# A two-layer hybrid diffusion trunk on one core: first norm's modulation split nine tiles on TensorE and seven rows on VectorE, later rows moved, out projection's low parts on GpSimd

## The chip, the core and the metric

One core of a Trainium2 chip runs the whole program in one launch. The metric is the device time in microseconds (us) of one execution; the median of three executions of the kernel before is 3165.7 us (3162.52 to 3169.48).

## The reference, cut to what matters

Two trunk layers act on 1024 latent tokens and 256 context tokens of width 1024. In each layer a conditioning vector is put through silu and a 1024 x 6144 matrix. It gives six vectors of 1024: shift, scale and gate of the mixing sub-layer, and shift, scale and gate of the MLP. Latent tokens use `c`, context tokens use `c_ctx`, with the same matrix.

```
mod   = split(silu(c)     @ w_mod[i] + b_mod[i], 6)     # sh1 sc1 ga1 sh2 sc2 ga2
mod_c = split(silu(c_ctx) @ w_mod[i] + b_mod[i], 6)
h = rmsnorm(x, g_pre_mix) * (1 + sc1) + sh1
u = h @ w_in                   # short conv | latent attention | conformer conv | 2-D attention
x = x + ga1 * rmsnorm(concat(mixers(u)) @ w_out, g_post_mix)
hm = rmsnorm(x, g_pre_mlp) * (1 + sc2) + sh2
x = x + ga2 * rmsnorm(square(relu(hm @ w_mlp1)) @ w_mlp2, g_post_mlp)
```

## The kernel before, in words

Activations lie with features on the 128 partitions and tokens along the free axis, in three segments: latents 0 to 511 (segment 0), latents 512 to 1023 (segment 1) and the context (segment 2, 256 tokens). Every large product is made in three passes (`mm3`, L125): high weight by high activation, high by low, low by high. The weight's high part is made by ScalarE (`hilo`, L101), its low part by a subtraction (L102) that goes to VectorE or to GpSimd. `weights` (L104) chooses by a counter: `eng = nc.vector if self.wcount % 4 < self.walt else nc.gpsimd`. `self.walt` is 0 except in the output projections: `WALT[0]` holds for the two halves of segment 0's projection in each layer (L1063 to L1069), `WALT[1]` for those of segments 1 and 2 of layer 0 and the end of the first MLP there (L1090 to L1108).

**The modulation of layer 0.** The 6144 outputs are 48 groups of 128, here called rows: 0 to 7 the shift, 8 to 15 the scale and 16 to 23 the gate of the mixing norm, 24 to 47 the three of the MLP (its gate is 40 to 47). A row is made in one of three ways. `mod_pe` (L250) loads a 128 x 1024 tile of 512 KB and multiplies it on TensorE by both vectors, two columns wide, in eight matmuls (L258). `mod_rows` (L286) loads the transposed weights in halves of 256 KB and lets VectorE make one 128x512 product with accumulation (L300) for each half and each of the two vectors: four per row. `mod_whole` (L307) loads 512 KB at once; with two vectors it takes two 128x512 products (L319) and one of 128x1024 (L322). Its loads and products are pinned behind what was traced before them on their engine. `mod_rows` and `mod_whole` need the vectors on all partitions; `mod_vectors` (L265) makes them either by TensorE (a column of ones by a 4 KB row, L276, then silu, L277) or by a load that repeats the 4 KB row on all partitions, 512 KB of data, and a silu in place (L280, L282).

**The start** (`run`, L1175). Rows 0 to 6 (`MPE` = 7) are TensorE's and 7 to 15 VectorE's. `merge(self.mod_pe(early), (md, RM))` (L1233) runs them side by side. Behind the fifth tile (`MX` = 4) `early` loads segment 0, takes its sums of squares and its 1/rms, and loads the first weights. Segments 1 and 2 are loaded when row 15 has been written out in the program. The norm's scaling (`modulate`, L184: L200, L201, L202 for each of eight feature tiles) waits for rows 0 to 15 through `gains` (L338, L353).

**Layer 0** (`layer`, L1013). `merge(main, (other, rate), ...)` (L994) writes out the main generator's steps and, after each, steps of the others up to `rate` times the cost so far. Rows 16 to 47 (`moda`, L1025) go beside six stages in a row: segment 0's first projections together with the norms of segments 1 and 2 (`pend`), two gated projections, the values, the latent attention's projections and its heads. Beside them runs the 31-tap convolution (L442). Row loads use the tag `xl`, of three buffers. A list scheduler then orders each engine's queue by priority and by a simulated readiness, so an instruction can move ahead of the place where it was written. After the heads come attention and output projection of segment 0 (`outproj`, L889; norms `na`, `n2`), segments 1 and 2 in the same way, and the MLP. In the MLP of segments 1 and 2 (L1127) a generator `hn` runs beside the products: the last norm of segment 0 (`resa`), the 48 rows of layer 1 (`modc`, by `mod_whole`) and the first norm of layer 1.

All loads go out on SyncE's queue. The tag `s` has 20 buffers of 4 KB per partition, for modulation tiles first and for the normalized activations after.

Of the kernel before, what the change touches and what calls it, by code (L numbers as in the profile page):

```python
# [6 lines left out]
AF = mybir.ActivationFunctionType  # L7
# [19 lines left out]
HB = 2  # L27
QTAG = 'xl'
PA, PD = 0, 1
WALT = (3, 2)  # L30
MPE, RM, MX = 7, 1.0, 4
ROT0, ROT1, ROT2 = 'SGSGS', 'SGSGS', 'SGSGS'
RATES = dict(pend=(1.0, 1.0), cv=(1.0, 0.862), cp=(1.0, 0.6), hr=(1.0, 0.484), hc=(0.3, 0.3), hm=(0.313, 0.679), ma=(0.195, 0.26), mf=(0.5, 0.5), mv=(0.5, 1.04), cb=(1.0, 1.3), mp=(0.5, 0.5), ar=(0.392, 0.517), ac=(0.6, 0.8), ob=(0.65, 0.696), oc=(0.575, 0.65), od=(0.65, 0.26), on=(0.6, 0.522), mb=(1.0, 0.646), pr=(0.2, 0.2), pt=(0.805, 1.12), pn=(0.612, 1.5), pm=(1.5, 1.5), mn=(1.74, 2.0), mc=(0.29, 0.325), mt=(1.0, 0.6), en=(1.0, 1.0))
PADC = 15
CFW = PADC + LAT + PADC + CTX + PADC
T5 = 1328
# [33 lines left out]
class Kern:  # L70
# [176 lines left out]
        return self.tc.keep_in_program_order(ins)  # L247


    def mod_pe(self, load):  # L250

        nc = self.nc
        ps = self.ps("O", [P, MPE, 2])
        for m in range(MPE):
            raw = self.t([P, KT, P], "s")
            nc.sync.dma_start(raw, self.a["wmod0"][m])
            for k in range(KT):
                nc.tensor.matmul(ps[:, m, :], raw[:, k, :], self.sc[:, k, :], start=k == 0, stop=k == KT - 1)  # L258
            if m == MX:
                load()  # L260
            yield 1.0
        for v in range(2):
            nc.vector.tensor_tensor(self.mods[0][v][:, 0:MPE], ps[:, :, v], self.vec[:, 0, 0:MPE], op=ALU.add)

    def mod_vectors(self, tags, pe=False):  # L265

        nc = self.nc
        out = []
        for v in range(2):
            t = self.t([P, 2, 512], tags[v])  # L270
            if pe:
                row = self.t([1, 1024], "s")
                nc.sync.dma_start(row, self.a["crow"][v:v + 1, :])
                for h in range(2):
                    ps = self.ps("S")
                    nc.tensor.matmul(ps, self.ones[0:1, :], row[:, h * 512:(h + 1) * 512], start=True, stop=True)  # L276
                    nc.scalar.activation(t[:, h], ps, AF.Silu)  # L277
                out.append([t[:, 0], t[:, 1]])
                continue
            nc.sync.dma_start(t, self.a["crow"][v:v + 1, :].rearrange("v (h c) -> v h c", h=2)  # L280
                              .to_broadcast([P, 2, 512]))
            nc.scalar.activation(t, t, AF.Silu)  # L282
            out.append(Halves(t))
        return out
# [728 lines left out]
    def layer(self, l, H, pend):  # L1013

        last = l == 1
        R = {k: v[l] for k, v in RATES.items()}
        qsegs = (0, 1) if last else (0, 1, 2)
        bsegs = qsegs[1:]
# [3 lines left out]
        ch = self.chain  # L1022
        self.cf_open(0)
        self.cf_open(1)
        moda = self.mod_rows(0, 16, 48, self.vecs) if l == 0 else iter(())  # L1025
        first = ch(*[self.cf_gemm(l, H, (0,), j, j == 0 and l == 0) for j in range(2)], self.na_project(l, H, "NQ", M_NAQ, (0,)))
        if l:
            first = ch(first, self.na_project(l, H, "NK", M_NAK, (0,)))
        self.merge(first, (pend, R['pend']), (moda, R['ma']))
        self.go(pend)  # L1030
        self.merge(self.cf_gemm(l, H, bsegs, 0), (moda, R['mf']))
        conv = ch(*[self.cf_conv(l, qsegs, j) for j in range(2)])
        self.merge(self.cf_gemm(l, H, bsegs, 1), (conv, R['cb']), (moda, R['mf']))
        self.merge(self.values(l, H), (conv, R['cv']), (moda, R['mv']))
        self.mla_open()
        self.merge(self.mla_project(l, H, (0, 1, 2), qsegs), (conv, R['cp']), (moda, R['mp']))
        heads = self.mla_heads(l, qsegs)
        rest1 = ch(self.na_project(l, H, "NK", M_NAK, (1, 2) if l else (0, 1, 2)), self.na_project(l, H, "NQ", M_NAQ, bsegs))
        self.merge(heads, (rest1, R['hr']), (conv, R['hc']), (moda, R['hm']))
        self.go(moda)  # L1040
        self.rot = "G"
        self.yfalloc(0)
# [19 lines left out]
        HM = {}  # L1062
        self.walt = WALT[0]  # L1063
        self.merge(self.outproj(l, 0, 0, 256, y0), (attb, R['ob']))
# [45 lines left out]
        vecs = self.mod_vectors(("c5", "ah"))  # L1110
        modc = ch(self.mod_whole(1, 0, 16, vecs), self.mod_whole(1, 16, 48, vecs[:1]))
        HN = {}
        m = self.mlp(l, (1, 2), HM, "ah", {1: "c5", 2: "ya"}, [(1, 0, 512), (2, 0, 256)], nb)
# [4 lines left out]
            return t  # L1118

        def hn():  # L1120
            yield from resa
            yield from modc
            HN[0] = self.newh(512)
            yield from self.modulate(get0, 512, 1, "1", 0, HN[0], 0, tmp="T")

        hn = hn()
        self.merge(self.upto(m, "part"), (nb, R['mn']), (hn, R['mc']))  # L1127
        self.go(nb, hn)
        p1 = self.norm(self.macc[1], 1, 0, 512, l, "2", None, self.scr["XM"], xout, (1, "1", lambda: HN[1]), **free)
# [33 lines left out]
    @staticmethod  # L1163
    def stats(g):

        next(g)
        next(g)
# [7 lines left out]
    def run(self):  # L1175
        nc, tc = self.nc, self.tc
# [38 lines left out]
        def load(si, tag):  # L1215
            o, n = SEGS[si]
            X[si] = Seg(pools[tag], n, F32, tag, f"x{si}")
            for i, t in enumerate(X[si].tiles):
                kk = X[si].kk
                nc.sync.dma_start(t, a["xin"][:, i * kk:(i + 1) * kk, o:o + n])  # L1220

        self.vecs = self.mod_vectors(("ya", "ya"), True)
        md = self.mod_rows(0, MPE, 16, self.vecs, wtag="s")
        H, first = {}, []

        def early():
            load(0, "ah")
            g = self.modulate(X[0].k, 512, 0, "1", 0, lambda: H[0], 0, tmp="T")
            self.stats(g)
            first.append(g)  # L1230
            self.w0 = [self.weights(a["win"][0, m], D) for m in (M_CFG, M_CFA)]

        self.merge(self.mod_pe(early), (md, RM))  # L1233
        self.go(md)
        load(1, "c5")
        load(2, "ah")
# [2 lines left out]
        pend = self.chain(*[self.modulate(X[si].k, SEGS[si][1], 0, "1", int(si == 2), H[si], 0, ptag="O", tmp="T") for si in (1, 2)])  # L1239
        H, pend = self.layer(0, H, pend)  # L1240
# [104 lines left out]
```

## Time and profile before

| | us |
|---|---|
| median of 3 executions | 3165.7 |
| the profiled execution: device time | 3172.64 |
| the profiled execution: span, first to last instruction | 3170.7 |
| TensorE busy | 2962.9 (93%) |
| VectorE busy | 1978.2 (62%) |
| ScalarE busy | 1388.2 (44%) |
| GpSimd busy | 1095.1 (35%) |

A busy share over the whole span hides that the stages have different limits, so the stages are read one by one. A stage is a stretch of time; in its row the engines' busy times are compared with its length. In a row of the profile, L300 is line 300 of the kernel, `ma<-xl,ya` the tile written and the tiles read, and the releaser of an idle stretch is the work that ended last before the engine went on. The profiled execution is 6.9 us longer than the median, and what is added to or taken from it is taken to change the median by as much.

### The profile page before, as it was taken

Reading aid. Unit: us, or ns where it says so; the run is one execution under the profiler, and the core shown is the slowest. Engines: PE = TensorE matmul, PEld = TensorE weight load, DVE = VectorE, ACT = ScalarE, POOL = GpSimd, SP = SyncE. Lnnn points to the kernel's source line nnn. Section 1 sums busy time; section 2 is a strip of 40 time slices with the busy share of each in tenths; the row PEclk is TensorE's granted clock in tenths of the full one; section 3 lists DMA queues with packets and bytes.
Section 4 is the critical chain, followed back from the end, with each engine's and each line's share of the span. In section 5 each row is a group of like instructions: output and inputs, shape, how many; then the busy total and the mean of one; then the engine's idle time right before and its main releaser. Section 6 shows DMA issues by size and latency. Waiting matters only on the chain.

```text
span 3170.7 us, 45433 instructions
## 1 busy us (share of the span) xinstructions
PE 2962.9 (93%) x15720; PEld 2529.0 (80%) x15720; DVE 1978.2 (62%) x3964; ACT 1388.2 (44%) x2840; POOL 1095.1 (35%) x865
## 2 busy tenths in 40 slices
PE   7889889979999989999999998997889999999997
PEld 5777678878888888888888886876878788888886
DVE  8999555686663367566654788556766526344335
ACT  3313445676553355322222533555755434343332
POOL 1302113224544432333332512222324444444443
PEclk9889889989999999999999999998989999999998
DMA  7435423353542263534522534335534324234223
GB/s 265 153 121 190 123 60 104 113 158 100 153 122 97 97 200 100 177 116 168 185 81 80 173 108 165 101 84 138 172 89 148 104 97 143 97 104 139 94 97 103
DMA packets 273193, 405.77 MB, mean 128 GB/s; under 512 B 27074, under 2 KB 124354, under 8 KB 272964
## 3 DMA queue, kind: packets, MB, share of 16 engines
q1 hardware_dynamic: 272964, 402.87, 39.9%
q8 instruction: 125, 2.05, 0.3%
q14 instruction: 104, 0.85, 0.1%
HBM read 350.47 MB, written 52.30 MB: 127 GB/s over the span
## 4 chain that ended last, share of the span: by engine, by line
PE 76%; DVE 5%; DMA 3%; issue 2%; ACT 2%; SPq 1%; POOL 0%; DVEq 0%; ACTq 0%; POOLq 0%
PE G L130 12%; PE G L131 12%; PE G L132 12%; PE S L130 10%; PE S L132 9%; PE S L131 9%; PE T L715 3%; PE O L728 1%; PE O L727 1%; DMA ah<-KR 1%; PE S L849 1%; PE S L799 1%; PE S L798 1%; PE S L800 1%; DVE sm L685 1%
## 5 line engine op out<-in xcount | busy, mean ns | idle before, releaser
L102 POOL TENSOR_TENSOR wl<-raw,wh 128x512 fp32r<-128x512 f32 x676 | 916.4, 1358 | 1479.7 <-ACT wh L101 1358.5
L101 ACT ACTIVATE wh<-raw 128x512 fp32r<-128x512 f32 x752 | 473.0, 631 | 870.2 <-PE S L131 390.9
L130 PE MATMUL G<-h,wh 128*128 128x512 f32 (+1 forms) x1144 | 436.5, 382 | 3.9 <-ACT h L201 1.2
L131 PE MATMUL G<-h,wh 128*128 128x512 f32 (+1 forms) x1144 | 432.4, 378 | 4.4 <-DVE h L202 4.3
L132 PE MATMUL G<-h,wl 128*128 128x512 f32 (+1 forms) x1144 | 432.7, 378 | 0.2 <-POOL wl L102 0.2
L130 PE MATMUL S<-h,wh 128*128 128x512 f32 (+1 forms) x888 | 317.8, 358 | 2.5 <-ACT h L201 1.6
L132 PE MATMUL S<-h,wl 128*128 128x512 f32 (+1 forms) x888 | 316.0, 356 | 1.4 <-POOL wl L102 1.4
L131 PE MATMUL S<-h,wh 128*128 128x512 f32 (+1 forms) x888 | 315.4, 355 | 0.0
L699 POOL TENSOR_SCALAR ah<-ah,sm 128x1280 f32<-128x1280 f32 (+3 forms) x144 | 148.5, 1035 | 407.4 <-DVE sm L698 156.7
L969 DVE TENSOR_TENSOR ac<-ac,S 128x512 f32<-128x512 f32 (+1 forms) x345 | 210.0, 612 | 124.2 <-PE S L132 123.2
L130 PEld LDWEIGHTS G<-h,wh 128*128 128x128 f32 x1144 | 219.5, 192 | 43.3 <-ACT h L201 2.8
L131 PEld LDWEIGHTS G<-h,wh 128*128 128x128 f32 x1144 | 219.5, 192 | 42.9 <-DVE h L202 6.0
L132 PEld LDWEIGHTS G<-h,wl 128*128 128x128 f32 x1144 | 219.4, 192 | 39.0 <-issue 0.7
L102 DVE TENSOR_TENSOR pt<-T,pt 128x512 fp32r<-128x512 f32 (+1 forms) x280 | 169.4, 615 | 90.5 <-ACT pt L101 89.4
L969 DVE TENSOR_TENSOR ac<-ac,G 128x512 f32<-128x512 f32 (+1 forms) x263 | 167.6, 637 | 79.1 <-PE G L132 77.6
L101 ACT ACTIVATE pt<-T 128x512 fp32r<-128x512 f32 (+1 forms) x280 | 146.8, 543 | 117.7 <-PE T L715 104.9
L130 PEld LDWEIGHTS S<-h,wh 128*128 128x128 f32 x888 | 170.8, 192 | 27.9 <-ACT h L201 2.3
L132 PEld LDWEIGHTS S<-h,wl 128*128 128x128 f32 x888 | 170.2, 192 | 27.4 <-POOL wl L102 2.6
L131 PEld LDWEIGHTS S<-h,wh 128*128 128x128 f32 x888 | 170.4, 192 | 24.7 <-issue 0.5
L130 PE MATMUL G<-s,wh 128*128 128x512 f32 (+1 forms) x532 | 184.4, 348 | 2.2 <-ACT ge L903 1.7
L132 PE MATMUL G<-s,wl 128*128 128x512 f32 (+1 forms) x532 | 181.1, 341 | 3.6 <-DVE wl L102 3.5
L131 PE MATMUL G<-s,wh 128*128 128x512 f32 (+1 forms) x532 | 181.6, 342 | 0.3 <-DVE s L102 0.3
(335 smaller groups left out, 6830.6 us busy)
## 6 DMA issues: line engine op xcount, KB each, us to landing
raw<-in_w_dram SPq DMA_DIRECT2D x520, 256.0 KB, 2.5
raw<-in_wout_dram SPq DMA_DIRECT2D x128, 256.0 KB, 3.0
raw<-in_win_dram SPq DMA_DIRECT2D x96, 256.0 KB, 3.0
s<-in_wmodt_dram SPq DMA_DIRECT2D x48, 512.0 KB, 4.2
xl<-in_wmodt_dram SPq DMA_DIRECT2D x64, 256.0 KB, 2.6
ah<-KN SPq DMA_DIRECT2D x32, 320.0 KB, 5.0
ah<-MV SPq DMA_DIRECT2D x16, 640.0 KB, 6.5
ah<-NV SPq DMA_DIRECT2D x16, 640.0 KB, 4.9
```

The source lines that it names most:

```text
L101: nc.scalar.activation(hi, src, AF.Copy)
L102: (eng or nc.vector).tensor_tensor(lo, src, f32(hi), op=ALU.subtract)
L130: nc.tensor.matmul(out, wh, xh, start=i == 0, stop=False)
L131: nc.tensor.matmul(out, wh, xl, start=False, stop=False)
L132: nc.tensor.matmul(out, wl, xh, start=False, stop=i == last)
L685: nc.vector.tensor_reduce(sm[:, i:i + 1], s, op=ALU.max, axis=AX.X)
L699: nc.gpsimd.tensor_scalar(p[:, :L], p[:, :L], sm[:, 9:10], 1.0, op0=ALU.mult, op1=ALU.mult)
L715: nc.tensor.transpose(T[:, i, q * P:(q + 1) * P], ps_list[q][:, cols[q]:cols[q] + P], self.ident)
L727: nc.tensor.matmul(O[:, a:b], V[:, kt, :], th[:, i, a:b], start=first, stop=False)
L728: nc.tensor.matmul(O[:, a:b], V[:, kt, :], tl[:, i, a:b], start=False, stop=last)
L798: nc.tensor.matmul(S, Qt[:, 0, q:q + P], K[0][:, ks], start=True, stop=False)
L969: nc.vector.tensor_tensor(a, a, ps, op=ALU.add)
```

## The change

- `MPE` goes from 7 to 9: rows 7 and 8 move from VectorE to TensorE. Segment 0 is loaded behind the third tile (`MX` = 2) and its statistics and the first weights come behind the seventh (`MS` = 6). `RM`, the rate of the row work beside the tiles, goes from 1.0 to 1.9.
- The two vectors are made by the repeating load and a silu in place, and no more by TensorE.
- `moda` covers rows 16 to 39 and starts behind `first` and `pend`, at the rates of `MODA`. Rows 40 to 47 are made by `mod_whole` in `hn`, ahead of `resa`. The rate `mc` of `hn` goes from 0.29 to 0.33.
- `WALT` goes from (3, 2) to (1, 0): of four low parts of a weight, one instead of three is VectorE's in segment 0's projections, none instead of two in those of segments 1 and 2.

```diff
-WALT = (3, 2)
-MPE, RM, MX = 7, 1.0, 4
+WALT = (1, 0)
+MPE, MX, MS, RM = 9, 2, 6, 1.9
+MODA = (0.8, 0.4, 0.4, 0.4, 0.2)
...
-    def mod_pe(self, load):
+    def mod_pe(self, steps):
...
-            if m == MX:
-                load()
+            if m in steps:
+                steps[m]()
...
-    def mod_vectors(self, tags, pe=False):
+    def mod_vectors(self, tags):
...
-            if pe:
-                row = self.t([1, 1024], "s")
-                nc.sync.dma_start(row, self.a["crow"][v:v + 1, :])
-                for h in range(2):
-                    ps = self.ps("S")
-                    nc.tensor.matmul(ps, self.ones[0:1, :], row[:, h * 512:(h + 1) * 512], start=True, stop=True)
-                    nc.scalar.activation(t[:, h], ps, AF.Silu)
-                out.append([t[:, 0], t[:, 1]])
-                continue
...
-        moda = self.mod_rows(0, 16, 48, self.vecs) if l == 0 else iter(())
+        moda = self.mod_rows(0, 16, 40, self.vecs) if l == 0 else iter(())
...
-        self.merge(first, (pend, R['pend']), (moda, R['ma']))
+        self.merge(first, (pend, R['pend']))
         self.go(pend)
-        self.merge(self.cf_gemm(l, H, bsegs, 0), (moda, R['mf']))
+        self.merge(self.cf_gemm(l, H, bsegs, 0), (moda, MODA[0]))
         conv = ch(*[self.cf_conv(l, qsegs, j) for j in range(2)])
-        self.merge(self.cf_gemm(l, H, bsegs, 1), (conv, R['cb']), (moda, R['mf']))
-        self.merge(self.values(l, H), (conv, R['cv']), (moda, R['mv']))
+        self.merge(self.cf_gemm(l, H, bsegs, 1), (conv, R['cb']), (moda, MODA[1]))
+        self.merge(self.values(l, H), (conv, R['cv']), (moda, MODA[2]))
...
         def hn():
+            yield from self.mod_whole(0, 40, 48, vecs)
             yield from resa
             yield from modc
...
-        def early():
-            load(0, "ah")
+        def stats():
             g = self.modulate(X[0].k, 512, 0, "1", 0, lambda: H[0], 0, tmp="T")
             self.stats(g)
             first.append(g)
             self.w0 = [self.weights(a["win"][0, m], D) for m in (M_CFG, M_CFA)]
...
-        self.merge(self.mod_pe(early), (md, RM))
+        self.vecs = self.mod_vectors(("ya", "ya"))
+        md = self.mod_rows(0, MPE, 16, self.vecs, wtag="s")
+        self.merge(self.mod_pe({MX: lambda: load(0, "ah"), MS: stats}), (md, RM))
```

The stages of the projections and heads use `MODA[3]` and `MODA[4]` (0.4 and 0.2) where 0.5 and 0.313 stood. In the table of rates, besides `mc`, only entries that are no longer used are left out.

## Rows read from the trace of the kernel before

**Rows 1.** Busy us by stage: length, PE, PEld, DVE, ACT, POOL, clock, DMA share, GB/s

```profile
0.00:20.00 20.00, 15.92 (x48) 10.85 (x48) 7.75 (x24) 6.68 (x11) 0.41 (x5) 1.00 0.89 308
20.00:56.00 36.00, 21.09 (x93) 19.46 (x92) 35.15 (x94) 11.89 (x22) 6.89 (x5) 1.00 0.89 328
56.00:120.00 64.00, 51.40 (x179) 35.93 (x180) 63.97 (x138) 29.04 (x48) 23.38 (x14) 0.91 0.46 152
120.00:320.00 200.00, 177.69 (x968) 154.00 (x967) 195.62 (x439) 51.38 (x115) 31.89 (x22) 0.93 0.45 152
```

**Rows 2.** Order of time: start, us; end of rows 7 to 15, and the first product

```profile
52.31 0.15 DVE L353 SCALAR_TENSOR_TENSOR g<-mod,vec 128x8 f32<-128x8 f32 x1
...
55.98 0.80 PE L415 MATMUL S<-h,wh 128*128 128x512 f32 x1 [0.93 <-ACT h L201]
```

**Rows 3.** Order of time, VectorE: the last row product and the next idle time

```profile
329.79 0.69 DVE L300 SCALAR_TENSOR_TENSOR xl<-xl,ya 128x512 f32<-128x512 f32 x1
...
335.33 0.69 DVE L102 TENSOR_TENSOR pt<-G,ge 128x512 fp32r<-128x512 f32 x1 [4.25 <-ACT ge L101]
```

**Rows 4.** Groups on VectorE, 0 to 340 us: busy us, mean ns, idle before

```profile
L300 DVE SCALAR_TENSOR_TENSOR ma<-xl,ya 128x512 f32<-128x512 f32 x64 | 53.4, 834 | 4.3 <-DMA xl<-in_wmodt_dram 4.1
L300 DVE SCALAR_TENSOR_TENSOR xl<-xl,ya 128x512 f32<-128x512 f32 x64 | 49.9, 780 | 0.0
```

**Rows 5.** Order of time, VectorE: two row products back to back

```profile
45.19 0.69 DVE L300 SCALAR_TENSOR_TENSOR s<-s,ya 128x512 f32<-128x512 f32 x1
...
45.80 0.69 DVE L300 SCALAR_TENSOR_TENSOR ma<-s,ya 128x512 f32<-128x512 f32 x1
```

**Rows 6.** The two ways of making the vectors: duration ns min/median/max; landing

```profile
L276 PE MATMUL S<-s,ones x8: 1056/1056/1218, 4.1 to 14.0; 1*128 1x512 f32 x8
...
DMA to landing us min/median/max: 3.8/3.8/3.8
```

**Rows 7.** Groups on VectorE in the MLP, 1300 to 1780 us; then that stage's busy us

```profile
L322 DVE SCALAR_TENSOR_TENSOR s<-s,c 128x1024 f32<-128x1024 f32 x32 | 42.8, 1345 | 0.0
L319 DVE SCALAR_TENSOR_TENSOR ma<-s,c 128x512 f32<-128x512 f32 x32 | 28.8, 901 | 0.0
...
1300.00:1780.00 480.00, 479.92 (x2738) 419.42 (x2737) 295.54 (x565) 134.46 (x249) 175.82 (x120) 1.00 0.37 125
```

**Rows 8.** The page's groups: high and low parts of the weights, whole span

```profile
L102 POOL TENSOR_TENSOR wl<-raw,wh 128x512 fp32r<-128x512 f32 x676 | 916.4, 1358 | 1479.7 <-ACT wh L101 1358.5
L101 ACT ACTIVATE wh<-raw 128x512 fp32r<-128x512 f32 x752 | 473.0, 631 | 870.2 <-PE S L131 390.9
```

**Rows 9.** The chain that ended last: VectorE's low parts on it

```profile
663.24 0.68 DVE wl L102
664.85 1.69 DVE wl L102
...
1171.20 0.59 DVE wl L102
...
1174.40 0.99 DVE wl L102
...
2263.05 0.60 DVE wl L102
...
2267.93 0.61 DVE wl L102
```

**Rows 10.** Order of time: four subtractions on GpSimd, and VectorE's work meanwhile

```profile
90.45 5.97 POOL L102 TENSOR_TENSOR wl<-raw,wh 128x512 fp32r<-128x512 f32 x4 [1.11 <-ACT wh L101]
...
90.22 0.74 DVE L202 SCALAR_TENSOR_TENSOR h<-T,mod,h 128x512 fp32r<-128x512 f32 x1
...
93.50 1.77 DVE L300 SCALAR_TENSOR_TENSOR ma<-xl,ya 128x512 f32<-128x512 f32 x1
```

**Rows 11.** Projections of segments 1, 2: GpSimd's group 1100 to 1270 us; busy us

```profile
L102 POOL TENSOR_TENSOR wl<-raw,wh 128x512 fp32r<-128x512 f32 x41 | 53.7, 1317 | 112.6 <-ACT wh L101 105.9 <-PE S L132 4.0 <-DVE yo L233 1.9
...
1120.00:1140.00 20.00, 20.00 (x172) 20.00 (x171) 9.72 (x14) 13.07 (x29) 8.59 (x7) 1.00 0.58 186
```

More of the change, by code (lines that the diff above doesn't have):

```diff
@@ L29 @@
 PA, PD = 0, 1
-WALT = (3, 2)
-MPE, RM, MX = 7, 1.0, 4
+WALT = (1, 0)
+MPE, MX, MS, RM = 9, 2, 6, 1.9
+MODA = (0.8, 0.4, 0.4, 0.4, 0.2)
 ROT0, ROT1, ROT2 = 'SGSGS', 'SGSGS', 'SGSGS'
-RATES = dict(pend=(1.0, 1.0), cv=(1.0, 0.862), cp=(1.0, 0.6), hr=(1.0, 0.484), hc=(0.3, 0.3), hm=(0.313, 0.679), ma=(0.195, 0.26), mf=(0.5, 0.5), mv=(0.5, 1.04), cb=(1.0, 1.3), mp=(0.5, 0.5), ar=(0.392, 0.517), ac=(0.6, 0.8), ob=(0.65, 0.696), oc=(0.575, 0.65), od=(0.65, 0.26), on=(0.6, 0.522), mb=(1.0, 0.646), pr=(0.2, 0.2), pt=(0.805, 1.12), pn=(0.612, 1.5), pm=(1.5, 1.5), mn=(1.74, 2.0), mc=(0.29, 0.325), mt=(1.0, 0.6), en=(1.0, 1.0))
+RATES = dict(pend=(1.0, 1.0), cv=(1.0, 0.862), cp=(1.0, 0.6), hr=(1.0, 0.484), hc=(0.3, 0.3), cb=(1.0, 1.3), ar=(0.392, 0.517), ac=(0.6, 0.8), ob=(0.65, 0.696), oc=(0.575, 0.65), od=(0.65, 0.26), on=(0.6, 0.522), mb=(1.0, 0.646), pr=(0.2, 0.2), pt=(0.805, 1.12), pn=(0.612, 1.5), pm=(1.5, 1.5), mn=(1.74, 2.0), mc=(0.33, 0.325), mt=(1.0, 0.6), en=(1.0, 1.0))
 PADC = 15
@@ L1028, in layer @@
             first = ch(first, self.na_project(l, H, "NK", M_NAK, (0,)))
-        self.merge(first, (pend, R['pend']), (moda, R['ma']))
+        self.merge(first, (pend, R['pend']))
         self.go(pend)
-        self.merge(self.cf_gemm(l, H, bsegs, 0), (moda, R['mf']))
+        self.merge(self.cf_gemm(l, H, bsegs, 0), (moda, MODA[0]))
         conv = ch(*[self.cf_conv(l, qsegs, j) for j in range(2)])
-        self.merge(self.cf_gemm(l, H, bsegs, 1), (conv, R['cb']), (moda, R['mf']))
-        self.merge(self.values(l, H), (conv, R['cv']), (moda, R['mv']))
+        self.merge(self.cf_gemm(l, H, bsegs, 1), (conv, R['cb']), (moda, MODA[1]))
+        self.merge(self.values(l, H), (conv, R['cv']), (moda, MODA[2]))
         self.mla_open()
-        self.merge(self.mla_project(l, H, (0, 1, 2), qsegs), (conv, R['cp']), (moda, R['mp']))
+        self.merge(self.mla_project(l, H, (0, 1, 2), qsegs), (conv, R['cp']), (moda, MODA[3]))
         heads = self.mla_heads(l, qsegs)
         rest1 = ch(self.na_project(l, H, "NK", M_NAK, (1, 2) if l else (0, 1, 2)), self.na_project(l, H, "NQ", M_NAQ, bsegs))
-        self.merge(heads, (rest1, R['hr']), (conv, R['hc']), (moda, R['hm']))
+        self.merge(heads, (rest1, R['hr']), (conv, R['hc']), (moda, MODA[4]))
         self.go(moda)
@@ L1220, in load @@
                 nc.sync.dma_start(t, a["xin"][:, i * kk:(i + 1) * kk, o:o + n])
-        self.vecs = self.mod_vectors(("ya", "ya"), True)
-        md = self.mod_rows(0, MPE, 16, self.vecs, wtag="s")
         H, first = {}, []
-        def early():
-            load(0, "ah")
+        def stats():
             g = self.modulate(X[0].k, 512, 0, "1", 0, lambda: H[0], 0, tmp="T")
```

## The prediction, made before the changed kernel ran

> **What bounds the kernel now.** The busy shares of the whole span name TensorE, but they are an average, so I went to the table of busy times by stage. From 20 to 320 us VectorE is busy 294.7 of 300 us, while TensorE is busy 250.2 and its granted clock is below full speed in two of the three stages [rows 1]. So the first tenth of the program goes at VectorE's pace. The order of time says what that means at its two ends. The first product starts at 55.98 us, because the scale's gain, which needs rows 7 to 15, is only made at 52.31 [rows 2]. At the other end the last row product starts at 329.79, and from there VectorE has idle time before its instructions again [rows 3]. The grouping by line says what fills VectorE: rows 16 to 47 alone are 103.3 us of busy time in 128 products [rows 4]. Later stages are different: in the MLP of segments 1 and 2 TensorE is busy 479.92 of 480 us and VectorE 295.54 [rows 7]. The chain of work that ended last tells about the output projections: it passes through six low parts on VectorE [rows 9].
>
> **Part 1: row products leave the front.** Rows 7 and 8 are 8 products, rows 40 to 47 are 32: 40 of them go. The recorded durations overlap; two in a row start 0.61 us apart [rows 5], so what a product holds VectorE for is 0.61 us where nothing disturbs it: 40 x 0.61 = 24.4 us. The mean busy time with all disturbances is 103.3 / 128 = 0.81 us [rows 4], which makes 32.3 us the upper end. The lower end is 0, where VectorE would wait instead. I take 24.4, since VectorE is full before and after. The small additions behind each group of eight rows move along and are left out.
>
> What takes the place of rows 7 and 8 is 16 matmuls two columns wide, and two loads of 512 KB for four of 256 KB: the same bytes. TensorE has nothing else to do before 55.98. Cover gone, it would be as many us as the tiles land late, which the next part bounds.
>
> **Part 2: the start.** Eight matmuls of 1.056 us go [rows 6], and with them VectorE's waits for the vectors. Instead two loads of 512 KB stand first on SyncE's queue; such loads landed 3.8 us after issue in the one place where the kernel has them [rows 6]. They put 1 MB ahead of everything behind them, x of segment 0 and every row included: at the 308 GB/s of the first stage [rows 1] that is 3.4 us. Ahead of x the bytes hardly change: five tiles and five half rows (3.75 MB) become three tiles, four half rows and the vectors (3.5 MB).
>
> How soon can the gain be made? By the program's order, nine tiles (4.5 MB), 14 half rows (3.5), x (2), the vectors (1) and the first weights (1) must land, 12 MB. At 308 GB/s up to 20 us and 328 after [rows 1] that is 20 + 5.8 / 0.328 = 38 us. VectorE has 28 products and the seven additions of the sums of squares in this time, some 22 us, so loads now set the start, and the first product comes near 41 us instead of 56. This is not added to the sum: VectorE's work after it is the same, and it is VectorE's total that ends the front. What counts is its idle time before the gain: 12.3 us up to 20 us now [rows 1], about 38 - 22 - 1 = 15 then. I take 2 us of loss (bounds: 3 us gained if the loads keep their order, 5 lost if the statistics, now behind the seventh tile, hold up the tiles behind them on TensorE's queue).
>
> **Part 3: later rows behind the norms.** Rows 16 to 39 are still 96 products, and only their order changes; 48 half-row loads instead of 64 go through the three buffers and SyncE's queue. With VectorE always occupied the order costs nothing. If there are gaps, it does (first rival). Number: 0, from 0 to the whole 24.4.
>
> **Part 4: eight rows in the MLP.** A row there is two products of 0.90 and one of 1.345 us [rows 7], 3.15 us, and eight are 25.2 us. TensorE covers them: VectorE has 184 us free in 480 [rows 7]. Without that cover it would be all 25.2. SyncE gets eight loads of 512 KB, pinned, each waiting for an `s` buffer, with MLP weights queued behind it; layer 1's 48 such loads already run in this stage with TensorE never idle [rows 7]. The residual of segment 0 comes later by eight rows. The costs written in `hn`'s steps grow from 126 to 145 (1.15 times) and its rate by 0.33 / 0.29 = 1.14, so the end of the first norm of layer 1 stays where it was. I take 0, from 0 to 6 us (a quarter of the rows uncovered).
>
> **Part 5: low parts to GpSimd.** 752 high parts stand against 676 low parts on GpSimd [rows 8], so VectorE has 76: 24 in segment 0 of each layer and 28 in segments 1 and 2 of layer 0. The change leaves 8, 8 and 0, so 60 move. Six of the 76 lie on the chain that ended last, 5.16 us in all [rows 9]; 60 / 76 of that is 4 us. GpSimd's queue gets 60 x 1.36 = 82 us more [rows 8], in stages where it idles over half of the time [rows 11]. I take 4 us gained, from 8 gained to 10 lost.
>
> While GpSimd subtracts, a row product on VectorE takes 1.77 us instead of 0.69, while an operation that reads one of its inputs from PSUM keeps 0.74 [rows 10, 5]. The Trainium skill ("GPSIMD Engine Reference", section Key points) says as much: the two engines share their SBUF interfaces, and GpSimd contends with VectorE instructions that have two SBUF inputs. By that rule part 5 could lose, which the fourth rival prices from the rows.
>
> **Sum.** -24.4 + 2 + 0 + 0 - 4 = -26.4 us. The profiled execution of 3172.6 us would become 3146.2; it lies 6.9 us above the median, and against the median the forecast is 3165.7 - 26.4 = 3139.3 us.
>
> **The rivals.** *First: the rows were filler, and the gain stays in VectorE's gaps.* From 56 to 120 us rows share VectorE with the norms of segments 1 and 2, each a chain through ScalarE and TensorE. With no row among them VectorE may wait for that chain, and rows that filled the waits come later. The point is 24 us of idle time on VectorE between the gain and 120 us. For it speaks that the new order starts rows only behind the norms; against it that the scheduler moves ready work forward, and that the evacuations of segment 0's products are there to fill gaps. Half to all of the gain is lost: about 3155 to 3165, say 3160.
>
> *Second: the gain is larger.* The 40 products are worth 32.3 us, the start loses nothing, the norm stages gain 8 instead of 4: 3165.7 - 40 = 3125. For it speaks the mean of 0.81 us; against it that GpSimd's work in the front stays, and would disturb other instructions instead.
>
> *Third, slower: GpSimd sets the pace of the output projections of segments 1 and 2.* There 192 matmuls of a half go at 172 in 20 us [rows 11], 22.3 us, and all 16 low parts would be GpSimd's: 16 x 1.317 = 21.1 us. It decides where three halves lose more than the 26.4 us gained, at (22.3 + 8.8) / 16 = 1.94 us each. With 1.77 us, the duration to which VectorE's own product is drawn out by sharing [rows 10], the halves lose 18 us; at 2.5 us they lose 53, and the time is 3139 + 53 = 3192. Against it speaks the mean of 1.317 with VectorE working beside it; for it, that four in a row took 1.49 each [rows 10].
>
> *Fourth: VectorE pays for the moved parts.* If each of the 60 holds up a VectorE instruction by 1.77 - 0.69 = 1.08 us [rows 5, 10] on the way to the end, that is 64.8 us for 36.6 us saved (60 x 0.61): 28 us lost instead of 4 gained, 3171. Against it: in the projections of segments 1 and 2 most of VectorE's operands are in PSUM.
>
> **Chances.** Forecast 0.49, first rival 0.17, second 0.19, third 0.10, fourth 0.05. A measurement of this kernel can tell about 0.2% (6.3 us) from no change. Faster by more: forecast, second, and half of the first, 0.76. Within: the other half of the first and a little of the fourth, 0.10. Slower: 0.14. The range leaves out the third and fourth rival's times and a tail of the second: from 3112 (27 us below the forecast, with 40 products at 0.81, part 5 at its better end and the start three us ahead, and a clock that no longer falls) to 3163.
>
> **What would show it.** Right: the gain (L353) near 38 us, the first product near 41; VectorE full from there to about 305, with the last row product of layer 0's front there; eight more L322 rows in the MLP with TensorE at full; segment 0's attention starting some 22 us earlier; norm stages after the projections a little shorter. The first rival shows as idle time on VectorE up to 120 us, the third as TensorE waiting for `wl` from GpSimd from 1080 to 1220 us, the fourth as longer `yo` and `pt` operations. I am wrong if the front's end does not move by at least 15 us, or if what it wins is lost again in a stage that the change touches.

## The result, and the profile after

The changed kernel takes 3149.1 us (median; 3145.2 to 3150.4) where the kernel before, run beside it, takes 3167.6: the ratio is 0.9937 (95% interval 0.9925 to 0.9949), 20 us less by that ratio (16 to 24; the medians differ by 18.5). The profiled execution took 3145.2 us with a span of 3143.3. It is 27.4 us below the profiled execution of before, but that one was long: the unchanged kernel ran between 3157.8 and 3174.0 us in 23 executions, so a difference of a few us between two single executions says nothing by itself.

First the table of busy times by stage, after the change; columns as in [rows 1], with a last row that answers to the MLP row of [rows 7] and, before it, one of segments 1 and 2's projection, [rows 11].

```profile
0.00:20.00 20.00, 8.95 (x42) 8.98 (x43) 6.52 (x19) 5.86 (x8) 0.41 (x5) 1.00 0.89 310
20.00:56.00 36.00, 31.28 (x127) 28.28 (x127) 31.49 (x80) 15.69 (x25) 7.11 (x6) 1.00 0.93 348
56.00:120.00 64.00, 53.88 (x223) 41.71 (x221) 62.39 (x142) 28.45 (x51) 22.38 (x15) 0.89 0.48 154
120.00:300.00 180.00, 165.70 (x911) 143.69 (x912) 177.32 (x382) 50.44 (x113) 31.01 (x22) 0.94 0.45 149
300.00:320.00 20.00, 11.44 (x56) 8.63 (x55) 8.66 (x16) 6.21 (x13) 3.81 (x3) 0.87 0.53 169
...
1100.00:1120.00 20.00, 20.00 (x172) 20.00 (x171) 6.42 (x6) 12.78 (x29) 18.13 (x15) 1.00 0.62 186
1280.00:1760.00 480.00, 478.45 (x2731) 417.60 (x2730) 307.29 (x582) 136.67 (x252) 172.43 (x118) 1.00 0.42 136
```

VectorE is now full to 300 us instead of 320, and after that it is busy for 8.66 of 20 us. The MLP took the eight rows in with TensorE at 478.45 of 480 us.

The order of time on TensorE and VectorE, the end of the start; it answers to [rows 2].

```profile
28.71 10.38 PE L259 MATMUL O<-sc,s 128*128 128x2 f32 x48
38.95 2.05 PE L179 MATMUL G<-e,ones 128*128 128x512 f32 x2
40.80 6.83 PE L259 MATMUL O<-sc,s 128*128 128x2 f32 x32
...
41.49 0.69 DVE L292 SCALAR_TENSOR_TENSOR s<-s,ya 128x512 f32<-128x512 f32 x1
...
47.66 0.24 DVE L264 TENSOR_TENSOR mod<-O,vec 128x9 f32<-128x9 f32 x2
47.87 0.24 DVE L345 SCALAR_TENSOR_TENSOR g<-mod,vec 128x8 f32<-128x8 f32 x2
49.60 0.80 PE L407 MATMUL S<-h,wh 128*128 128x512 f32 x1 [1.98 <-ACT h L202]
```

The first product starts at 49.60 us; it was 55.98. VectorE's last product of the start is over at 42.2, but TensorE is at work without a gap from 28.71 to 47.63: five tiles (L259), and the statistics of segment 0 (L179) between them. What makes nine tiles take so long shows in the view of that line (duration in ns min/median/max, first and last start):

```profile
L259 PE MATMUL O<-sc,s x144: 213/353/371, 11.1 to 47.3; 128*128 128x2 f32 x144
```

144 records stand for nine tiles, 16 for each, although a tile is eight matmuls in the code. The last 32 of them take 6.83 us: 3.4 us of TensorE for each tile. The kernel before has the same 16 records for each of its seven tiles:

```profile
L258 PE MATMUL O<-sc,s x112: 352/353/375, 9.5 to 37.0; 128*128 128x2 f32 x112
```

Next VectorE in order of time, which answers to [rows 3]: the last row product of the front, and the next idle times.

```profile
220.04 0.68 DVE L292 SCALAR_TENSOR_TENSOR xl<-xl,ya 128x512 f32<-128x512 f32 x1
...
296.79 0.69 DVE L103 TENSOR_TENSOR pt<-e,ge 128x512 fp32r<-128x512 f32 x1 [1.77 <-ACT ge L102]
...
299.52 0.69 DVE L103 TENSOR_TENSOR pt<-G,ge 128x512 fp32r<-128x512 f32 x1 [0.72 <-ACT ge L102]
...
303.65 0.42 DVE L103 TENSOR_TENSOR pt<-S,ge 128x256 fp32r<-128x256 f32 x1 [2.50 <-ACT ge L102]
```

The last row product of the front starts at 220.04 us instead of 329.79 [rows 3]. Behind it VectorE is kept busy by the convolution, whose last instruction starts at 297.4.

Last, the page's group of low parts on GpSimd (it answers to [rows 8]) and, in a second fence, the low parts on the chain that ended last ([rows 9]). The third fence is the one of GpSimd's on the chain of before, which [rows 9] does not have.

```profile
L103 POOL TENSOR_TENSOR wl<-raw,wh 128x512 fp32r<-128x512 f32 x736 | 996.8, 1358 | 1414.7 <-ACT wh L102 1352.1
```

```profile
1122.33 1.02 POOL wl L103
2146.38 1.30 POOL wl L103
2242.13 0.60 DVE wl L103
2255.34 1.28 POOL wl L103
2263.74 1.46 POOL wl L103
```

```profile
2336.73 1.36 POOL wl L102
```

60 low parts have moved, as the prediction counted. The chain still runs through low parts of both engines: 5.66 us after, 6.5 before with [rows 9]. In a second execution of each kernel it is 9.1 us after and 8.8 before, so the low parts on the chain of one execution are no steady amount.

**Where the lead is.** The same event is taken in both traces, and the time of after is subtracted from that of before. "Again" is a second profiled execution of each kernel.

| event | lead, us | lead, again |
|---|---|---|
| first product (L415 before) | 6.4 | 7.0 |
| VectorE's last instruction of the convolution (L442) | 28.2 | 32.8 |
| first output of segment 0's attention (L740) | 24.4 | 26.0 |
| last output of it | 28.4 | 28.0 |
| 16th output of the projection behind it | 21.3 | 22.3 |
| start of segment 1's projection (L903) | 19.8 | 20.2 |
| layer 1, first instruction of the convolution | 19.4 | 18.9 |
| end of the span | 27.4 | 20.2 |

So the lead is won in the front of layer 0. Of it 6 to 7 us go between 577 and 650 us, in segment 0's projection, and 20 us last to the end. The last row of the first column is the long execution of before.

### The profile page after: what moved, and what is told of

Its sections match the earlier page's. It is cut to its first block, busy times and chain, and to the rows that moved or that the text cites. A ratio compares the mean times of both kernels' runs of the same rounds, so it can differ in the third digit from the quotient of the medians.

```text
span 3143.3 us, 45430 instructions
## 1 busy us (share of the span) xinstructions
PE 2954.6 (94%) x15744; PEld 2531.6 (81%) x15744; DVE 1953.1 (62%) x3867; ACT 1390.1 (44%) x2838; POOL 1174.1 (37%) x925
## 3 DMA queue, kind: packets, MB, share of 16 engines
q8 instruction: 125, 2.05, 0.3%
## 4 chain that ended last, share of the span: by engine, by line
PE 69%; DVE 6%; DMA 2%; ACT 1%; issue 1%; SPq 1%; POOL 0%; DVEq 0%; ACTq 0%; POOLq 0%
PE G L131 11%; PE G L132 11%; PE G L133 11%; PE S L131 9%; PE S L133 9%; PE S L132 9%; PE T L707 2%; PE O L720 1%; PE O L719 1%; PE S L790 1%; PE S L841 1%; PE S L791 1%; PE S L792 1%; DVE T L434 1%; DVE pt L103 1%
## 5 line engine op out<-in xcount | busy, mean ns | idle before, releaser
L103 POOL TENSOR_TENSOR wl<-raw,wh 128x512 fp32r<-128x512 f32 x736 | 996.8, 1358 | 1414.7 <-ACT wh L102 1352.1
L691 POOL TENSOR_SCALAR ah<-ah,sm 128x1280 f32<-128x1280 f32 (+3 forms) x144 | 147.1, 1024 | 398.2 <-DVE sm L690 170.4
L132 PEld LDWEIGHTS G<-h,wh 128*128 128x128 f32 x1152 | 218.9, 190 | 39.6 <-DVE h L203 1.6
```

What stands on the lines that cost most here:

```text
L103: (eng or nc.vector).tensor_tensor(lo, src, f32(hi), op=ALU.subtract)
L132: nc.tensor.matmul(out, wh, xl, start=False, stop=False)
L691: nc.gpsimd.tensor_scalar(p[:, :L], p[:, :L], sm[:, 9:10], 1.0, op0=ALU.mult, op1=ALU.mult)
```

## The experiments

The theory: VectorE's total sets the end of the front, so the eight rows that leave it (and rows 7 and 8) are the gain, the MLP hides them, and the low parts add some. Rivals: the earlier start or the new order is the gain, TensorE's own progress ends the front, the low parts cost or give more. Each ratio is to the kernel before, run beside it.

### The low parts alone, and all but the low parts

```diff
-WALT = (3, 2)
+WALT = (1, 0)
```

The first has this edit alone, in the kernel before; the second undoes it in the changed kernel.

> The kernel before with the share of the low parts alone changed: 60 of VectorE's 76 low parts go to GpSimd. Theory (the prediction's part 5: VectorE's low parts lie on the chain that ended last for 5.16 us, and 60 of 76 leave it): about 4 us faster, between 0 and 8, with GpSimd's 60 more subtractions hidden. Rival A (each moved part holds up VectorE instructions by more than it saves, or GpSimd falls behind): 3 to 10 us slower; in the two profiles segment 0's attention ends 28 us earlier after the change, but by the first MLP's middle only 20 us are left, and segment 0's second projection half is the first place where the lead shrinks. It would show as the evacuations of that half coming later than in the kernel before.

> The changed kernel with the old share of the low parts, so the whole change but this part. Theory (low parts worth 4 us): 22 us faster than the kernel before, some 4 us slower than the whole change. Rival A (low parts cost 3 to 10 us): 22 to 29 us faster than before, that is faster than the whole change, and the lead of 28 us at the end of segment 0's attention is carried through the first MLP.

Measured: 3165.0 us, ratio 0.9993 (0.9982 to 1.0004), and 3147.6 us, 0.9939 (0.9923 to 0.9954). Alone the part does nothing that can be measured, and the change without it is worth the same. The interval (6 us gained to 1 lost) still has room for the forecast's 4 us, but none for the loss of the third or fourth rival.

### The eight rows alone, and the eight rows put back

To the kernel before only the following was added; the other kernel undoes it in the changed kernel (rows 16 to 47 in the front, the last rate of `MODA` 0.48, `mc` 0.29).

```diff
-        moda = self.mod_rows(0, 16, 48, self.vecs) if l == 0 else iter(())
+        moda = self.mod_rows(0, 16, 40, self.vecs) if l == 0 else iter(())
...
         def hn():
+            yield from self.mod_whole(0, 40, 48, vecs)
             yield from resa
```

(and `mc` 0.33 for 0.29)

> The kernel before with rows 40 to 47 alone moved into the MLP: 32 row products leave the front. Theory (VectorE's total sets the front's end, 0.61 us for a product): 19.5 us faster, between 15 and 26, and attention's first output (yput) earlier by as much; the MLP hides the moved rows. Rival B (the start decides: the first product's earlier time and the rows on TensorE bring the gain): under 8 us. Rival C (the moved rows are not hidden in the MLP): the lead at attention's first output is 19.5 us, and the end's lead is smaller by up to 25 us.

> The changed kernel with rows 40 to 47 back in the front (the rate beside the heads raised from 0.2 to 0.48 to hold them), so that the start, the order and the low parts are all that is changed. Theory: 8 row products less than before are worth 4.9 us, the start loses 2 and the low parts gain 4: 7 us faster than before, between 0 and 12. Rival B (the start decides): 18 us or more faster, near the whole change.

Measured: 3152.9 us, 0.9953 (0.9939 to 0.9967), 15 us less than before; and 3161.4 us, 0.9982 (0.9971 to 0.9992), 6 us less. Taken out of the change, the eight rows cost 14 us; alone they give 15, which the total time cannot tell from the 20 of the whole change (the intervals overlap). The traces can: at the start of layer 1 the eight rows alone lead by 8.5 us and the whole change by 19.4. The rest of the 15 us is won in layer 1, of which this kernel edits no line: from its first instruction of the convolution to the end of the span it took 1302 us, and 1313 and 1310 in the two traces of before. And the traces show what the theory has no place for. With the eight rows alone, VectorE is done with the convolution 26.8 us earlier, nearly as early as after the whole change (28.2), while attention's first output comes only 10.6 us earlier, not 24.4. Its stages by busy time (columns as above):

```profile
280.00:300.00 20.00, 19.68 (x105) 16.54 (x104) 17.98 (x34) 8.22 (x17) 3.87 (x3) 1.00 0.52 178
300.00:320.00 20.00, 17.51 (x99) 14.57 (x98) 9.40 (x15) 8.55 (x16) 6.33 (x5) 0.97 0.66 215
320.00:340.00 20.00, 12.47 (x39) 9.41 (x39) 5.81 (x12) 3.80 (x9) 1.26 (x1) 0.69 0.63 175
```

From 300 us VectorE idles over half of the time, and TensorE is busy 17.51 of 20 us: it still has products of the front to make. The changed kernel is at 11.44 there. The opposite case is the kernel with the rows put back, in the same view:

```profile
300.00:320.00 20.00, 12.26 (x51) 10.14 (x50) 19.15 (x36) 5.67 (x11) 3.02 (x3) 0.73 0.47 161
```

Here TensorE waits and VectorE is full. The front has two ends, and both must come earlier.

### The order alone, and the start alone

The first changes, in the kernel before, only the rates of row work beside the stages; the second has the changed kernel's start with the old order, rates, `WALT` and all 32 rows in the front.

```diff
-        self.merge(first, (pend, R['pend']), (moda, R['ma']))
+        self.merge(first, (pend, R['pend']))
...
-        self.merge(self.cf_gemm(l, H, bsegs, 0), (moda, R['mf']))
+        self.merge(self.cf_gemm(l, H, bsegs, 0), (moda, 0.8))
...
-        self.merge(heads, (rest1, R['hr']), (conv, R['hc']), (moda, R['hm']))
+        self.merge(heads, (rest1, R['hr']), (conv, R['hc']), (moda, 0.48))
```

(the three rates between are 0.4)

> The kernel before with the order alone changed: no rows beside the norms of segments 1 and 2, all of rows 16 to 47 behind them at rates that hold them (0.8, 0.4, 0.4, 0.4, 0.48). VectorE's total is the same. Theory now (the front has two ends, VectorE's total and TensorE's own progress, and attention starts when both are done): the norms come earlier, TensorE is ahead by 120 us, but VectorE ends where it ended, so 0 to 5 us faster, and the last convolution step stays near 326 us. The prediction said 0. Rival (the order is what brings the 6 us of the run with eight rows back): 5 us or more faster.

> The changed start alone (nine tiles on TensorE, seven rows on VectorE, the repeating loads, x behind the third tile, statistics behind the seventh), with rows 16 to 47 in the old order at the old rates and the old share of the low parts. VectorE has 8 row products less than before. Theory: the first product comes 6 us earlier, at 50 us, VectorE's end moves by the 8 products less its longer idle time, so 3 to 5 us faster. Rival (the order brings the gain): 0 to 2 us faster.

Measured: 3162.0 us, 0.9977 (0.9967 to 0.9988), and 3161.0 us, 0.9977 (0.9968 to 0.9985), 7 us less each. For the order alone the trace gives no lead in the front: attention's first output is 8 us later than in the first trace of before, 7 than in the second. The stage of the norms:

```profile
56.00:120.00 64.00, 51.83 (x178) 36.74 (x179) 63.97 (x137) 28.93 (x49) 23.69 (x14) 0.86 0.48 151
```

VectorE is as full as in [rows 1]: the scheduler moved row products forward beside the norms, although they are written behind them. So TensorE is not ahead by 120 us, as had been expected. The kernel reaches layer 1 still 5.7 us late and ends its span 8.4 us ahead of the first trace of before and 3.6 ahead of the second. No line of layer 1 was edited, but the scheduler has put its queues in another order: 1008 of TensorE's 6183 instructions there stand at another place than before. What of this makes the gain stays open. The start alone has the first product 7 us earlier, VectorE's end 1.7 us later than in the first trace of before and 2.2 earlier than in the second, and attention 3.4 and 4.8 us earlier: the lead of the start hardly reaches the end of a front that VectorE sets.

### Rows made twice in the MLP, and eight rows left out of the front

The first makes rows 40 to 47 twice in the MLP of the changed kernel (`mc` 0.374), the second leaves rows 32 to 39 out.

```diff
         def hn():
+            yield from self.mod_whole(0, 40, 48, vecs)
             yield from self.mod_whole(0, 40, 48, vecs)
```

```diff
-        moda = self.mod_rows(0, 16, 40, self.vecs) if l == 0 else iter(())
+        moda = self.mod_rows(0, 16, 32, self.vecs) if l == 0 else iter(())
...
+        if l == 0:
+            for v in range(2):
+                self.nc.vector.tensor_copy(self.mods[0][v][:, 32:40], self.vec[:, 0, 32:40])
```

> The changed kernel with rows 40 to 47 made twice in the MLP (the same values; the rate of the work beside the MLP raised from 0.33 to 0.374 to hold them), 25 us of VectorE's time more. Theory (TensorE covers the rows there): the time of the changed kernel, 18 to 20 us below the kernel before, no more than 2 us later. Rival (the moved rows cost some of what they won): 3 us or more later than the changed kernel, and the moved rows would then have cost about as much themselves.

> The changed kernel without the products of rows 32 to 39 (the scale of the first MLP's norm is its bias alone), so 32 row products less in the front. Theory (TensorE's own progress has become the front's second end): well under the 14 us that the first eight rows were worth, 3 to 10 us faster than the changed kernel, with VectorE idle from about 275 us. Rival (VectorE's total still sets the front alone): 15 to 20 us faster than the changed kernel, some 35 to 40 below the kernel before. Third (TensorE alone sets it now): 0 to 2 us.

Measured: 3149.1 us, 0.9938 (0.9925 to 0.9950), the time of the changed kernel with 27 us more of VectorE's products in the MLP (60.4 + 42.9 us in its groups, 44.6 + 31.7 in those of the change): the rows there are hidden, with room. And 3143.3 us, 0.9919 (0.9906 to 0.9932), 26 us less than before and some 6 less than the change, which is just clear of noise; attention's first output comes 5.4 us earlier than in the change. 32 more products of 0.61 us, 19.5 us, have left the front and 5 to 6 come out. Its stages by busy time show why:

```profile
260.00:280.00 20.00, 20.00 (x107) 16.88 (x106) 14.42 (x26) 7.56 (x16) 4.08 (x3) 1.00 0.60 202
280.00:300.00 20.00, 18.47 (x106) 15.48 (x104) 8.41 (x14) 8.38 (x16) 6.30 (x5) 1.00 0.59 203
```

VectorE has time to spare from 260 us on, with TensorE busy for 20.00 and 18.47 of 20 us: now the front ends with TensorE.

### Each kernel once more

Both kernels unchanged, for a second trace.

> The kernel before, profiled a second time. In its first profile segment 0's output projection and norms in layer 1 (2250 to 2370 us) end some 7 us later against their own start than in all eight other kernels, four of which run the same share of low parts there. Theory: that was one execution, and this one has those 7 us less there, so a span of some 3164 us. Rival (every execution of this kernel loses them there, so that any edit that reorders the queues wins 7 us): the same delay again.

> The changed kernel, profiled a second time. In its first profile the lead over the kernel before is 29 us at the end of segment 0's attention and 20 us from segment 1's projection on. Theory (the order of the queues, the same in every execution, loses 9 us between the two): the same leads within 3 us. Rival (one execution's luck): a lead of 25 us or more kept to the end.

Measured: 3167.9 and 3147.6 us. They give the last column of the table of leads. The loss of 8 to 9 us between the end of segment 0's attention and segment 1's projection is in both pairs, so it belongs to the kernel and not to an execution. The second trace of before is 1.6 us ahead of the first at layer 1's start and 4.8 at the end: about 3 us of its layer 1, where some 7 were expected, were of that one execution.

### Fewer tiles on TensorE

If TensorE's tiles set the start, one or two tiles fewer should bring the gain earlier.

```diff
-MPE, MX, MS, RM = 9, 2, 6, 1.9
+MPE, MX, MS, RM = 8, 2, 6, 2.4
```

(and 7, 2, 6, 3.1)

> The changed kernel with eight tiles on TensorE instead of nine and eight rows on VectorE (the rate of the row work 2.4 instead of 1.9). In the changed kernel's profile VectorE is done with its rows at 42.3 us, while TensorE works off tiles from 28.7 to 47.6, 16 records of 0.217 us for a tile. Theory (TensorE's queue of tiles sets the start): one tile less is 3.5 us, one row more 2.4, so the gain at 44 to 45 us instead of 47.9, and the whole 0 to 3 us faster than the changed kernel. Rival (the loads set it, as the prediction had it): the gain stays within 1 us of 47.9.

> The changed kernel with seven tiles on TensorE and nine rows on VectorE, as before (the rate 3.1), all else changed. Theory (TensorE's queue or VectorE's, whichever ends last): TensorE would end at 41, VectorE at 47, so the gain at 46 to 48, again some 5 us ahead of the kernel before, which then is won by the repeating loads and the order of the loads alone; the time is that of the changed kernel, at most 4 us more. Rival (the tiles on TensorE are what brings the start): the gain near 52, and 4 us or more lost.

Measured: 3161.6 us, 0.9981 (0.9971 to 0.9992), and 3154.7 us, 0.9948 (0.9933 to 0.9963). By the ratios that is 14 us slower than the change with eight tiles, and 3 to 4 with seven, which is within the noise; between 3 us faster and 4 slower had been expected. At the start of layer 1 both are some 10 us behind the change. The earlier gain did come. With seven tiles it is at 46.07 us, against 52.31 in the kernel before, which has seven as well: the repeating loads and the order of the loads bring the start forward without the two rows on TensorE, and with these two it comes 1 to 2 us later (47.87, and 47.08 in the second trace of the change). With eight tiles the gain is at 44.56 and the first product at 48.15 (order of time):

```profile
36.04 2.06 PE L179 MATMUL G<-e,ones 128*128 128x512 f32 x2
37.88 6.83 PE L259 MATMUL O<-sc,s 128*128 128x2 f32 x32
...
44.56 0.28 DVE L345 SCALAR_TENSOR_TENSOR g<-mod,vec 128x8 f32<-128x8 f32 x2
...
48.15 0.80 PE L407 MATMUL S<-h,wh 128*128 128x512 f32 x1 [3.44 <-ACT h L202]
```

But the lead does not last. The stage from 100 to 120 us, first of the changed kernel, then with eight tiles, then with seven:

```profile
100.00:120.00 20.00, 15.46 (x68) 11.56 (x68) 20.00 (x61) 8.05 (x14) 1.12 (x2) 0.83 0.53 173
```

```profile
100.00:120.00 20.00, 13.41 (x40) 8.51 (x39) 20.00 (x61) 7.91 (x12) 0.41 (x1) 0.66 0.49 161
```

```profile
100.00:120.00 20.00, 11.50 (x24) 6.00 (x23) 19.97 (x59) 7.09 (x10) 1.16 (x1) 0.50 0.48 155
```

VectorE is full in all three, and TensorE gets 68, 40 and 24 matmuls done, with a granted clock that falls from 0.83 to 0.50. What it waits for is in the waits of this stretch (98 to 121 us: total, times, longest), again of the change, of eight tiles and of seven:

```profile
PE G L132 <- DVE h L203: 0.8, 1, 0.8
```

```profile
PE G L132 <- DVE h L203: 2.9, 2, 2.6
```

```profile
PE G L132 <- DVE h L203: 10.2, 6, 3.4
```

`h` from L203 is the last step of the norm, and each feature tile of it lets TensorE go on with three matmuls. With seven tiles VectorE makes it there between row products (order of time):

```profile
108.00 0.75 DVE L201 SCALAR_TENSOR_TENSOR T<-x,g,O 128x512 f32<-128x512 f32 x1
108.67 0.74 DVE L203 SCALAR_TENSOR_TENSOR h<-T,mod,h 128x512 fp32r<-128x512 f32 x1
109.33 0.68 DVE L292 SCALAR_TENSOR_TENSOR xl<-xl,ya 128x512 f32<-128x512 f32 x1
...
110.01 0.68 DVE L292 SCALAR_TENSOR_TENSOR ma<-xl,ya 128x512 f32<-128x512 f32 x1
110.65 0.75 DVE L201 SCALAR_TENSOR_TENSOR T<-x,g,O 128x512 f32<-128x512 f32 x1
```

A tile of the norm takes 2.65 us (108.00 to 110.65), half of it two row products that nobody waits for yet. From 56 to 120 us the change makes 18 of the L203 instructions, eight tiles 14 and seven 12, at nearly the same number of row products (39, 40, 41). So VectorE being full is not enough: what it makes first decides when TensorE can go on. Why the order tips so far for one tile is the scheduler's affair and was not taken apart. Seven tiles, behind at 120 us, cost less in the end than eight, but not by the front: at the start of layer 1 the two are 1.4 us apart. In layer 1, where their TensorE queues have the same order, one took 1301 us and the other 1310; why is not known.

### What the front's end follows

The columns that TensorE has been given by a time are counted from the matmul records.

| kernel | by 120 us, thousand | by 300 us | VectorE's end | attention's first output |
|---|---|---|---|---|
| before | 94.2 | 409.2 | 325.6 | 393.9 |
| before, again | 94.2 | 399.0 | 329.5 | 395.3 |
| low parts alone | 93.7 | 399.5 | 330.6 | 398.9 |
| eight rows alone | 94.2 | 416.4 | 298.8 | 383.4 |
| start alone | 107.3 | 420.3 | 327.3 | 390.6 |
| change, rows put back | 105.3 | 428.8 | 325.2 | 387.9 |
| change, eight tiles | 97.8 | 417.7 | 296.6 | 380.1 |
| change, seven tiles | 88.8 | 416.4 | 303.8 | 381.6 |
| change | 108.3 | 435.9 | 297.4 | 369.5 |
| change, again | 109.4 | 437.2 | 296.7 | 369.4 |
| change, rows 32 to 39 left out | 109.4 | 442.6 | 270.2 | 364.1 |

The first three rows, kernels with the front of before, tell the noise: 10 thousand columns at 300 us, and 5 us in the last two columns. By attention's first output each kernel has been given nearly the same number of columns, 534 to 539 thousand, so a kernel that is behind at 300 us has that much more to do until then.

Four kernels have VectorE's end between 297 and 304 us, and attention in three of them starts 11 to 14 us after that of the change. What those three lack is 18 to 20 thousand columns of TensorE's by 300 us. With eight rows alone TensorE gets 41 thousand columns in the full 20 us up to 300, so 18 to 20 thousand are 9 to 10 us: most of the difference. Two have TensorE ahead at 120 us and VectorE's end where it was, and win 3 to 6 us against the first trace of before, 5 to 7 against the second.

## Why the prediction came out as it did

The sign and the range were right (3112 to 3163 us, measured 3149), and the forecast's mechanism is in the main the one that won: row products left a front that VectorE filled. The size was 26.4 us and is 20 (16 to 24). The front's end moved by more than the 15 us that were set as the least. But part of that was lost again in a stage that the change touches, which stood as a sign of being wrong too: the sum has no term for the 8 to 9 us given back behind segment 0's attention.

**Part 1, row products leave the front: right in size by luck, short in reason.** 24.4 us were taken from 40 products, and attention starts 24.4 us earlier (26.0 in the second pair). Two errors cancel here. A product that leaves is worth more than 0.61 us: 32 fewer moved VectorE's end by 26.8 us (eight rows alone) and by 27.2 (rows 32 to 39 left out of the change), 0.84 and 0.85 us each, near the mean of 0.81 [rows 4] that stood as the upper end. And attention does not follow VectorE's end by itself: eight rows alone gave 10.6 us there. The step that failed is the sentence that the earlier first product is not added to the sum because it is VectorE's total that ends the front. TensorE's own queue of products ends it as well. Only with the start, which put TensorE 14 thousand columns ahead by 120 us, did VectorE's end, 28.2 us earlier, move attention by 24.4.

**Part 2, the start: the time was wrong.** The gain was forecast near 38 us and came at 47.87, the first product near 41 and came at 49.60. The failed step is that TensorE has nothing else to do before the first product, so that the tiles cost nothing. Two tiles more were counted as 16 matmuls; the trace has 32 records, 6.83 us. The trace of before could have told: it has 112 records for seven tiles, and [rows 6] has eight (L276) for the four matmuls of the code. TensorE is busy for 31.28 of the 36 us up to 56 [rows 1 had 21.09], and the statistics behind the seventh tile hold up the last two for 2.05 us, which was named as a bound. The loads, which the forecast took as the limit, had given VectorE its last row by 42.2. The tiles are not all of the miss, as eight of them still have the gain at 44.56; and 38 us would have been 39.6 if the sum had taken its 12 MB in the same units as its 3.4 us for 1 MB. The 2 us of loss were mis-sized as well: VectorE idles 18.0 of the first 56 us, 13.1 before [rows 1], so 4.9 us, at the bound of 5 that was given.

**Part 3, the order: 0 as predicted in the front,** where the order alone moved nothing forward. VectorE is busy 62.39 of 64 us up to 120, so the first rival, gaps in place of the rows, falls. The last row product was forecast near 305 us and starts at 220.04: the rows still go early, and what fills VectorE to 297 us is the convolution. What the first rival had right is that the order in which VectorE does its work counts, as the kernels with fewer tiles show.

**Part 4, eight rows in the MLP: right.** TensorE stays full, and doubling the rows changes nothing.

**Part 5, low parts: 4 us that did not show.** The step that failed is to price them as a share of 5.16 us on the chain of one execution: the chain still runs through low parts after the change, and their sum differs by 2 to 3 us between two executions of one kernel. A wait did go. In layer 1, at segment 0's projection (2130 to 2360 us), TensorE waits for a low part of VectorE's in both traces of before, in none of after:

```profile
PE G L132 <- DVE wl L102: 3.2, 1, 3.2
```

But the change with the old share has this wait too and takes the same time. The norm stages after the projections were to get shorter; the lead shrinks there instead. The third rival's sign is not there: between 1060 and 1230 us TensorE waits for no low part of GpSimd's (0.2 us in the second trace), and at 1100 us it makes 172 matmuls in 20 us with GpSimd busy 18.13 us. It was near: little room is left there. The second rival's 8 us do not show either.

The row products that stay do collide with GpSimd, as [rows 10] had shown. In the start, in order of time:

```profile
32.08 6.13 POOL L103 TENSOR_TENSOR wl<-raw,wh 128x512 fp32r<-128x512 f32 x4 [31.14 <-ACT wh L102]
...
37.02 1.74 DVE L292 SCALAR_TENSOR_TENSOR ma<-s,ya 128x512 f32<-128x512 f32 x1
```

Four subtractions take 1.53 us each and a product beside them 1.74 instead of 0.69. This agrees with the Trainium skill ("GPSIMD Engine Reference", section Key points), which lets the two engines contend where a VectorE instruction reads two inputs from SBUF. The fourth rival, which priced the moved parts by the rows at 28 us lost, falls with the low parts alone at 0.9993: in the projections no such loss reached the end. Its sign is not there either: from 1060 to 1230 us the `yo` and `pt` operations take 681 and 663 ns, 682 and 648 before.

**What was given back.** From 28 us at the end of segment 0's attention the lead falls to 20 us. With the old share of low parts it is still 29.2 us at the 16th output of the projection, then 23.0 at segment 1's and 20.9 at layer 1, and the time is the same in the end. So the low parts decide where the loss shows, and hardly how large it is. Which of the reordered queues makes it is open: no test removed one of them. A kernel with rows 32 to 39 made later, beside attention, was not tried. Of the kernels that compute everything none beat the change. Two equal it (the old share of low parts, the rows made twice), and two more, seven tiles and the eight rows alone, lie within the noise of it.

## What to carry over

When one engine is full through a stage, ask what the next engine still has to do when that one is done: here VectorE done 27 us earlier was worth 11 us at attention's start, and 28 us earlier was worth 24 with TensorE's products started earlier. Do not price an operation by its time on the critical chain of one execution: here that time differed by 2 to 3 us between two executions of one kernel, and moving the operations to another engine showed no gain. And read a step's price on the engine that takes it over from that engine's own records, not from its number of instructions in the code.

## What was not expected of the hardware

- In these traces a matmul of f32 operands is recorded twice: 144 records for 72 in the code with two columns, eight for four with 512 [rows 6]. A tile of 128 x 1024 takes 3.4 us, and nine tiles hold TensorE for 31 us (9 x 3.46).
- A row order that does nothing in the stages it was written for still moved the whole kernel by 7 us (0.9977), and one tile less on TensorE by 14 us (0.9981 against 0.9937). Here a gain of 7 us was no evidence for the reason one had for it.
- Layer 1, counted as above, took between 1299 and 1313 us in the fourteen traces, though no kernel edits more of it than the share of low parts. Two executions of the same kernel differ there by 3.1 us (before) and 3.6 us (after).
- GpSimd took 60 more subtractions (736 instead of 676) at an unchanged mean of 1358 ns.
